# Row norms of an encoder layer gathered and spread by transposes instead of 32-bit matmuls, and two bank copies placed behind a third

## The chip, the cores and the metric

The kernel runs on one core of one Trainium2 chip. The metric is the device time of one launch in microseconds (us); for the kernel before there are three timed runs, with a median of 1317.9 us (1316.01 to 1318.08). One more execution was recorded by the hardware profiler. Engines in the profile: PE (the matrix engine, with its weight loads as PEld), DVE (vector), ACT (scalar), POOL (GpSimd) and SP (whose queue issues nearly all DMAs).

## The reference

One layer of an encoder, 1024 tokens of width 1024, in 32-bit floats. Cut to what matters here:

```
def rms_norm(x, g):
    y = x * rsqrt(mean(x * x, axis=-1) + 1e-6)
    return y * g

h = rms_norm(x, norm_mix)
q_a, k_a, v_a, q_b, k_b, v_b, g_a, g_b = split(h @ w_in)
o_a = neighbourhood_attention(...)      # 8 heads of 64
o_b = sliding_window_attention(...)     # 8 heads of 64, 2 key/value heads
y = sigmoid(g_a) * (o_a @ w_branch_a) + sigmoid(g_b) * (o_b @ w_branch_b)
x = x + y @ w_out
h = rms_norm(x, norm_ffn)
u = silu(h @ w_gate) * (h @ w_up)       # width 2816
x = x + u @ w_down
```

What the change touches are the two norms. Each needs one factor `rsqrt(mean + eps)` per token. The factor is not applied to `x` ahead of the matmul; it multiplies the product, whose tokens lie along the free axis of a tile, so that the factor must stand in all 128 partitions.

## The kernel before, in words

Activations are kept transposed: features in the 128 partitions, tokens along the free axis, in two halves of 512 tokens. A 32-bit product is made from three matmuls of a faster 32-bit type: each operand is split into a high and a low part (helper lines L50 and L51 for a plain split, L53 and L54 with a scale per partition; names end in h and l), and L824, L825 and L826 multiply high by high, high by low, low by high.

The stages follow one another on PE: projections, attention heads mixed with gate projections as filler, the other gates, the branch products, the output product (`out_pair`), the FFN's hidden blocks, the down product. From the gates on, a 2x2 block product is made of seven products instead of eight (class `Seven`, products named 1 to 7, taken in the order 1, 5, 6, 2, 7, 3, 4, and for the hidden blocks 0 and 1 in the order 1, 5, 6, 7, 3, 2, 4). The operand of a product p is a sum of weight blocks (s1 to s4, added by DVE at L806) that is then split; PSUM banks X, Y, Z and V (two sets, 0 and 1) accumulate it. When product 1 and then product 6 are done, ACT copies a bank into another (L828), from which later products go on.

**The norms.** `wide_rs` holds the factor for the 512 tokens of a half in all 128 partitions. For the first norm, the factors of all tokens come from ACT and POOL as columns `rows_rs` (128 tokens by 8). `wide_norm`, called twice within the filler, has DVE multiply the identity by each of four columns (`diag`), and PE multiply a tile of ones by the four diagonal matrices (L161); ACT copies the bank into `wide_rs`. For the second norm, `both_sums` (the same tile as `wide_rs`) holds squares summed over the 8 feature tiles; `ffn_norm` adds up its partitions with matmuls against one column of ones (L1227), DVE scales (L1229), POOL raises to the power -0.5 (L1230). `diagonal` and `spread_norm` (L1236, L1241) then do for it what `wide_norm` does for the first. On PE the gather stands behind product 6 of the hidden blocks 0 and 1, then come 24 matmuls of product 7 of both blocks into the banks Z, then the spread; bank V serves for the gathered sums and then for the spread factors.

**Hidden blocks.** `hidden(i)`, i from 0 to 21, makes 128 columns of the gate and of the up product for all tokens, two blocks at a time from i = 4. `p5` is a copy of bank V (after product 5), `c22` the sum of bank Z and `p5` (after product 7, L1364). DVE and ACT then apply the norm and the gating (`gated`, L1246 to L1248, and L1366 to L1370). From block 4 on, product 1 of a pair is itself made from seven products over quarters (`first_products`, L1318 to L1320; operands named sq, qa to qd, tokens q and qb), while product 5 of both blocks is woven in between, so that `hidden` is told that 5 is `given`. `first_products` ends with a copy of bank X of the second block into its bank Y (L1346), kept as `att["first"]`.

**What sets the order.** The order on PE is written out in the program. ACT, DVE, POOL and SP get theirs from the scheduler of the framework, which works with a simulated time line, except in an opening and in a stretch from the last output product to the spread of the second norm (`begin` to `change.close()`), where ACT and DVE also follow the program. `tc.issue_after(x)` makes the scheduler put what follows behind x. A small edit can therefore move rows on ACT, DVE and SP far from its own place.

Of the kernel before, what the change touches and what calls it, by code (L numbers as in the profile page):

```python
# [10 lines left out]
F32 = mybir.dt.float32  # L11
F32R = mybir.dt.float32r
AF = mybir.ActivationFunctionType
ALU = mybir.AluOpType
AX = mybir.AxisListType

T = 1024
D = 1024
# [3 lines left out]
EPS = 1e-6  # L22
# [3 lines left out]
def block_kernel(ctx, tc, x, xt, small, w_in, rpb, t5, w_ba, w_bb, w_out, w_gate, w_up, w_down,  # L26
                 onehot, swmask, namask, out):
    nc = tc.nc
    P = 128

    cst = ctx.enter_context(tc.tile_pool(name="cst", bufs=1))
    big = ctx.enter_context(tc.tile_pool(name="big", bufs=1))
    wp = ctx.enter_context(tc.tile_pool(name="wp", bufs=1))
# [23 lines left out]
    NWU = 8  # L57
# [29 lines left out]
    def half_cols(h):  # L87
        return slice(h * 512, h * 512 + 512)
# [3 lines left out]
    def halves(z):  # L92
        return z[:, LO], z[:, HI]
# [8 lines left out]
    def tok(t):  # L102
        return slice(t * P, (t + 1) * P)


    ident = cst.tile([P, P], F32, name="ident")
# [9 lines left out]

    ones = cst.tile([P, P], F32, name="ones")
    nc.gpsimd.memset(ones, 1.0)  # L120
    h = [[None, None] for k in range(8)]
    for e, c in ((0, 1), (0, 0), (1, 0), (1, 1)):
        for k in range(e, 8, 2):
# [3 lines left out]
    rows_rs = cst.tile([P, 8], F32, name="rows_rs")  # L127
# [18 lines left out]
    def row_norm(c):  # L146
# [5 lines left out]
        nc.gpsimd.tensor_scalar(rows_eps[:, d], rows_rs[:, d], HD * EPS, 1.0, op0=ALU.mult, op1=ALU.mult)  # L152
        nc.gpsimd.tensor_tensor(rows_rs[:, d], rows_rs[:, d], mhalf[:, 0:4], ALU.pow)

    def wide_norm(c, ps):

        dg = wp.tile([P, 512], F32, tag="whi", name=f"diag{c}", bufs=NWU)
        for j in range(4):
            nc.vector.tensor_scalar_mul(dg[:, tok(j)], ident, rows_rs[:, 4 * c + j:4 * c + j + 1])
        for j in range(4):  # L160
            nc.tensor.matmul(ps[:, tok(j)], ones, dg[:, tok(j)], start=True, stop=True)  # L161
        nc.scalar.copy(wide_rs[c], ps)

    def load_small():
# [61 lines left out]
    att = {}  # L226
# [230 lines left out]
    def filler(pending):  # L457
        for gi in range(1, len(order)):
            for i, cost in enumerate(projection(gi, weights[gi], pending, weights.get(gi + 1))):
                if gi == len(order) - 1 and i == 58:  # L460
                    wg = gate_weights(1, 0)
                yield cost
        todo = [(0, 1), (1, 1), (0, 0), (1, 0)]
        for i, (d, br) in enumerate(todo[:3]):
            def step(half, k):
                if i == 0 and not half and k in (1, 4):
                    wide_norm(k // 4, bank("pj", f"wide{k}"))
                if (i, half, k) == (1, 0, 0):
                    load_pair(0, slot_v, dma)
                at_step = 16 * i + 8 * half + k  # L470
                if at_step == 32:
                    load_pair(1, slot_v, dma)
                if at_step in range(26, 34) or at_step in range(40, 48):
                    if at_step in (26, 40):
                        j = at_step // 40
                        g22 = early.setdefault("g22", slot_u("g22h") if not j else None)
                        early[j] = row_sums(j, halves(g22)[j])
                    with tc.issue_after(att["bound"]):
                        next(early[at_step // 40])
                if (half, k) == (0, 7):  # L480
                    step.next = gate_weights(*todo[i + 1][::-1])
                if (half, k) in ((0, 6), (1, 3), (2, 1)):
                    pop(pending)
            yield from plain_gate(d, br, wg, step)
            wg = step.next
        last_gate.append(wg)
# [264 lines left out]
    def scratch(nm):  # L751
        return hp.tile([P, 512], F32, tag="S", name=nm, bufs=2)
# [4 lines left out]
    def scratch2(nm):  # L757
        return hp.tile([P, 1024], F32, tag="e4", name=nm, bufs=4)
# [14 lines left out]
    def bank_sets():  # L773

        return [{b: bank(t, f"bank{b}{i}") for b, t in zip("XYVZ", tags)}
                for i, tags in enumerate((("s", "pj", "s", "pj"), ("t", "pj", "t", "o")))]
# [130 lines left out]
    sets = bank_sets()  # L907
# [74 lines left out]
    sets = bank_sets()  # L982
# [13 lines left out]
    for n, (d, half) in enumerate(turns):  # L996
        j, c = d // 2, half_cols(half)
# [17 lines left out]
        if half == 0:  # L1015
            p = 2 if d % 2 else 1
# [37 lines left out]
    def prefetch_ffn(i):  # L1054

        if i >= NF:
            return prefetch_down(i - NF)
        st = [w_stage(f"wg{i}_"), w_stage2(f"wu{i}_")]
        for t, w in zip(st, (w_gate, w_up)):
            dma(t.rearrange("p (k c) -> p k c", c=P), w[0, :, tok(i)].rearrange("(k p) c -> p k c", p=P))  # L1060
        hid[i] = Seven(f"f{i}", [two(z) for z in st], 4, mx, sets)
# [28 lines left out]
    both_sums = wide_rs  # L1090
# [14 lines left out]
    def feed(*what):  # L1105

        for n, j in what:
            hi, lo = mx[BACK[n]][j]
            src, scale = raw_t[j][BACK[n]]
            split(hi, lo, src if kept(n, j) else f(lo), scale=scale)  # L1110
# [113 lines left out]
    def ffn_norm(half, ss):  # L1224

        for j in range(4):
            nc.tensor.matmul(ss[:, j:j + 1], both_sums[half][:, tok(j)], ones[:, 0:1], start=True, stop=True)  # L1227
        rs = hp.tile([P, 4], F32, tag="rs", name=f"rs{half}", bufs=2)
        nc.vector.tensor_scalar(rs, ss[:, 0:4], 1.0 / D, EPS, op0=ALU.mult, op1=ALU.add)  # L1229
        nc.gpsimd.tensor_tensor(rs, rs, mhalf[:, 0:4], ALU.pow)  # L1230
        return rs

    def diagonal(half, rs):
        dg = scratch(f"dg{half}")
        for j in range(4):
            nc.vector.tensor_scalar_mul(dg[:, tok(j)], ident, rs[:, j:j + 1])  # L1236
        return dg

    def spread_norm(half, dg, rb):
        for j in range(4):  # L1240
            nc.tensor.matmul(rb[:, tok(j)], ones, dg[:, tok(j)], start=True, stop=True)  # L1241
        nc.scalar.copy(rsb[half], rb)

    def gated(dst, src, half):

        nc.vector.tensor_mul(dst, src, rsb[half])  # L1246
        nc.scalar.activation(dst, dst, AF.Silu)  # L1247
        att["two"] = nc.vector.tensor_mul(dst, dst, rsb[half]).ins  # L1248
# [100 lines left out]
    def hidden(i, order=ORDER, given=()):  # L1349

        s = hid[i]
        us[i] = scratch2(f"u{i}")
        sg_lo, sg_hi = halves(us[i])
        p5, c22 = halves(scratch2(f"p5{i}"))
        y, z, v = (s.banks[b] for b in "YZV")
        for p in order:
            if p not in given:
                s.step(p)
            if p == 2:
                gated(sg_lo, s.banks["X"], 0)  # L1360
            elif p == 5:
                nc.scalar.copy(p5, v)
            elif p == 7:
                att["two"] = nc.vector.tensor_add(c22, z, p5).ins  # L1364
            elif p == 3:
                nc.vector.tensor_add(sg_hi, y, p5)  # L1366
                gated(sg_hi, sg_hi, 1)
            elif p == 4:
                nc.vector.tensor_mul(sg_lo, z, sg_lo)
                att["two"] = nc.vector.tensor_mul(sg_hi, c22, sg_hi).ins  # L1370
                if i % 2:
                    keep(i // 2, us[i - 1], us[i])
            if p == order[3]:
                prefetch_ffn(i + 2)
            yield p

    def keep(k, u0, u1):

        (b11, b12), (b21, b22) = halves(u0), halves(u1)
        t = TokenSums(f"u{k}", b11, b12, b22).rest(b21)  # L1380
        for n, p in enumerate(ORDER):
            row = (7 * k + n) * P
            nc.sync.dma_start(u_dram[row:row + P, :], t[p][0])

    ga, gb = (hidden(i, LAST2) for i in range(2))

    def both_blocks():
        next(ga)
        next(gb)
# [10 lines left out]
    for i, g in enumerate((ga, gb)):  # L1400
        prepare_ffn((i, 3))
        next(g)
    rs = [ffn_norm(half, sets[half]["V"]) for half in range(2)]
    feed(*((4, j) for j in range(4)))
    dg = [diagonal(half, rs[half]) for half in range(2)]
    both_blocks()
    prepare_ffn((0, 2), (1, 2))
    for half in range(2):
        spread_norm(half, dg[half], sets[half]["V"])
    feed(*((5, j) for j in range(4)))  # L1410
    change.close()
    in_turn(ga, gb)
# [1 line left out]
    for _ in hidden(2):  # L1414
        next(pieces)
    g = hidden(3)
    for p in g:
        next(pieces, None)
        if p == 3:
            break  # L1420
    for i in range(4, NF, 2):

        first = first_products(hid[i], hid[i + 1])
# [112 lines left out]
```

## Time and profile before

| | |
|---|---|
| timed runs | 1317.9, 1316.01, 1318.08 us |
| the profiled execution | 1317.18 us |
| its span, first to last instruction | 1315.2 us |
| mean granted clock of TensorE | 0.999 |
| PE busy | 1304.1 us, 99% of the span |
| DVE busy | 1018.6 us, 77% |
| ACT busy | 695.5 us, 53% |
| POOL busy | 182.8 us, 14% |

The span leaves out 2 us before the first and after the last instruction. Busy shares are averages: DVE is at nine tenths and more in some slices of the span and at half in others. Matmuls overlap in their pipeline, so a row of the time line gives the start of the first of a group, and the next row's start tells what the group cost.

### The profile page before, as it was taken

To read this page: it belongs to the slowest core of one execution; us is meant where nothing else is said; L and a number is where in the kernel's file an instruction comes from. 1 tells how busy PE (TensorE), PEld (TensorE's weight loads), DVE (VectorE), ACT (ScalarE), POOL (GpSimd) and SP (SyncE) were. 2 spreads that over 40 slices of the span, in tenths; PEclk is the share of its full clock that TensorE was granted. 3 is DMA by queue.
4 is the path that set the end of the run, shared out by engine and by line. 5 is a ranking of instruction groups with operands and counts; after the bars stand their busy time and mean duration, and the time that the engine had idled before them with its cause. 6 is when DMAs were issued, how large, how long until landed. Compare 5 with 4: busy or idle time off the path is not lost.

```text
span 1315.2 us, 19621 instructions
## 1 busy us (share of the span) xinstructions
PE 1304.1 (99%) x6618; PEld 1134.0 (86%) x6618; DVE 1018.6 (77%) x2039; ACT 695.5 (53%) x1459; POOL 182.8 (14%) x322
## 2 busy tenths in 40 slices
PE   9999999999999999999999999999999999999998
PEld 8999999999888888888888888888888888888887
DVE  5678867776687758879999878888777799697765
ACT  6677857776664225535556544443444455363532
POOL 1364645564310000000000000000000000000000
PEclk9999999999999999999999999999999999999999
DMA  9532424242535358657774533233233356672532
GB/s 311 147 89 61 110 62 109 61 135 64 143 118 184 122 158 275 216 188 220 253 235 120 168 105 106 87 104 117 80 109 121 120 171 221 240 248 65 184 121 88
DMA packets 180997, 191.92 MB, mean 146 GB/s; under 512 B 21104, under 2 KB 126576, under 8 KB 180896
## 3 DMA queue, kind: packets, MB, share of 16 engines
q1 hardware_dynamic: 180640, 190.57, 46.5%
q8 instruction: 52, 0.85, 0.3%
q14 instruction: 49, 0.40, 0.1%
q10 hardware_dynamic: 256, 0.10, 0.0%
HBM read 133.19 MB, written 52.37 MB: 141 GB/s over the span
## 4 chain that ended last, share of the span: by engine, by line
PE 84%; DMA 7%; DVE 5%; ACT 2%; issue 1%; SPq 1%; POOL 1%; POOLq 0%; ACTq 0%; DVEq 0%
PE bankZ L824 5%; PE bankZ L825 5%; PE bankZ L826 5%; PE bankY L824 5%; PE bankY L825 5%; PE bankY L826 5%; PE bankX L826 4%; PE bankX L824 4%; PE bankX L825 4%; PE pj L326 4%; PE pj L325 4%; PE pj L327 4%; PE o L649 3%; PE bankV L825 3%; PE bankV L824 3%; PE bankV L826 3%
## 5 line engine op out<-in xcount | busy, mean ns | idle before, releaser
L603 ACT ACTIVATE E<-E,nm 128x384 f32<-128x384 f32 (+3 forms) x128 | 75.7, 592 | 48.3 <-DVE nm L597 42.5
L605 POOL TENSOR_SCALAR E<-E,nm 128x384 f32<-128x384 f32 (+1 forms) x128 | 74.5, 583 | 95.0 <-DVE nm L604 71.0
L51 DVE TENSOR_TENSOR pl<-tp,ph 128x384 fp32r<-128x384 f32 (+1 forms) x128 | 66.4, 519 | 17.2 <-ACT ph L50 16.1
L50 ACT CAST ph<-tp 128x384 fp32r<-128x384 f32 (+1 forms) x128 | 57.4, 449 | 20.4 <-PE tp L615 19.9
L50 ACT CAST f<-f 128x512 fp32r<-128x512 f32 x87 | 50.9, 620 | 25.5 <-DMA f<-u_dram 24.9
L51 DVE TENSOR_TENSOR f<-f 128x512 fp32r<-128x512 f32 x87 | 56.4, 683 | 8.3 <-ACT f L50 8.1
L615 PE MATMUL tp<-ident,E 128*128 128x128 f32 x352 | 59.5, 272 | 0.9 <-POOL E L605 0.9
L615 PEld LDWEIGHTS tp<-ident,E 128*128 128x128 f32 x352 | 45.1, 140 | 5.9 <-POOL E L605 1.2
L345 POOL TENSOR_TENSOR ss<-ss,mhalf 128x4 f32<-128x4 f32 (+2 forms) x42 | 49.8, 1185 | 3.2
L649 PE MATMUL o<-pl,v 128*128 128x256 f32 (+2 forms) x160 | 48.7, 305 | 0.4 <-DVE pl L51 0.3
L604 DVE RECIPROCAL nm<-nm 128x1 f32<-128x1 f32 x128 | 20.4, 160 | 36.0 <-ACT E L603 34.6
L1230 POOL TENSOR_TENSOR rs<-rs,mhalf 128x4 f32<-128x4 f32 x2 | 2.8, 1419 | 319.1 <-DVE rs L1229 319.1
L649 PE MATMUL o<-ph,v 128*128 128x256 f32 (+2 forms) x160 | 45.9, 301 | 0.5 <-ACT ph L50 0.5
L591 PE MATMUL s<-k,q 128*128 128x384 f32 (+1 forms) x128 | 46.0, 359 | 0.0
L592 PE MATMUL s<-k,q 128*128 128x384 f32 (+1 forms) x128 | 41.4, 323 | 0.0
L597 DVE CUSTOM_DVE_ANT_0 E<-s,bsw,cols 128x384 f32<-128x384 f32 (+1 forms) x64 | 36.9, 577 | 4.6 <-PE s L592 3.9
L1247 ACT ACTIVATE u<-u 128x512 f32<-128x512 f32 x44 | 27.5, 629 | 19.7 <-DVE u L1246 19.6
L597 DVE CUSTOM_DVE_ANT_0 E<-s,bna 128x384 f32<-128x384 f32 (+1 forms) x64 | 32.9, 516 | 4.3 <-PE s L592 3.8
L824 PE MATMUL bankZ<-f,f_7h 128*128 128x512 f32 x88 | 35.0, 397 | 0.8 <-ACT bankZ L828 0.8
L1248 DVE TENSOR_TENSOR u<-u,wide_rs 128x512 f32<-128x512 f32 x44 | 30.0, 686 | 6.4 <-ACT u L1247 5.6
L826 PE MATMUL bankZ<-f,f_7l 128*128 128x512 f32 x88 | 34.7, 395 | 0.0
L825 PE MATMUL bankZ<-f,f_7h 128*128 128x512 f32 x88 | 34.7, 394 | 0.0
(1268 smaller groups left out, 4636.0 us busy)
## 6 DMA issues: line engine op xcount, KB each, us to landing
f<-u_dram SPq DMA_DIRECT2D x77, 256.0 KB
wg_s<-in_w_gate_dram SPq DMA_DIRECT2D x22, 512.0 KB
u_dram<-u SPq DMA_DIRECT2D x33, 256.0 KB
o_dram<-of SPq DMA_DIRECT2D x32, 256.0 KB
o<-o_dram SPq DMA_DIRECT2D x32, 256.0 KB
sg<-g_dram SPq DMA_DIRECT2D x32, 256.0 KB
g_dram<-go SPq DMA_DIRECT2D x24, 256.0 KB
u_dram<-tau SPq DMA_DIRECT2D x22, 256.0 KB
```

The costliest lines, as they stand in the source:

```text
L50: a = nc.scalar.copy(hi, src)
L51: b = (eng or nc.vector).tensor_tensor(lo, src, f(hi), ALU.subtract)
L325: nc.tensor.matmul(ps[:, :384], lh, his[k][:, :384], start=(k == 0), stop=False)
L326: nc.tensor.matmul(ps[:, :384], lh, los[k][:, :384], start=False, stop=False)
L597: att["bound"] = nc.vector.tensor_tensor_reduce(E[:, :n], s[:, :n], hd["bias"](qb), -1.0, sk if sw else 1e30, ALU.add, ALU.min, nm[:, 0:1] ...
L603: nc.scalar.activation(E[:, :m], E[:, :m], AF.Exp, bias=nm[:, 0:1], scale=-1.0, accum_out=nm[:, 1:2])
L605: nc.gpsimd.tensor_scalar(E[:, :n], E[:, :n], nm[:, 1:2], 1.0, op0=ALU.mult, op1=ALU.mult)
L615: nc.tensor.transpose(tp[:, tok(j)], hd["E"][qq][:, ko:ko + P], ident)
L649: nc.tensor.matmul(hd["O"][half][:, (a - half * 4) * P:(z + 1 - half * 4) * P], v[:, kb].rearrange("p a e -> p (a e)"), pp[:, (a - q0) * P ...
L824: nc.tensor.matmul(ps, hi[:, tok(j)], bh, start=first, stop=False, skip_group_check=True)
L825: nc.tensor.matmul(ps, hi[:, tok(j)], bl, start=False, stop=False, skip_group_check=True)
L826: nc.tensor.matmul(ps, lo[:, tok(j)], bh, start=False, stop=end, skip_group_check=True)
```

## The change

Three edits in the program.

1. The `ones` tile and its memset on POOL are gone. A new helper `spread` makes four 32-bit transposes: each takes one column of factors, read with stride 0 as a 128x128 matrix, so that the transpose puts the 128 factors of that column into every partition. `wide_norm` and `spread_norm` call it in place of diagonal matrices and matmuls. DVE's 8 `diag` and 8 `dg` multiplications are gone.
2. `ffn_norm` transposes the four 128x128 pieces of `both_sums` into the whole of bank V, and DVE adds up each 128 columns (`tensor_reduce`, 128x512 in, 128x4 out) ahead of the scaling. POOL's power stays.
3. In `hidden`, where product 5 is given (blocks 4 to 21), the copy of bank V into `p5` is issued after `att["first"]`.

```diff
-    ones = cst.tile([P, P], F32, name="ones")
-    nc.gpsimd.memset(ones, 1.0)
...
+    def spread(ps, rs):
+
+        for j in range(4):
+            nc.tensor.transpose(ps[:, tok(j)], rs[:, j:j + 1].to_broadcast([P, P]), ident)
+
     def wide_norm(c, ps):
 
-        dg = wp.tile([P, 512], F32, tag="whi", name=f"diag{c}", bufs=NWU)
-        for j in range(4):
-            nc.vector.tensor_scalar_mul(dg[:, tok(j)], ident, rows_rs[:, 4 * c + j:4 * c + j + 1])
-        for j in range(4):
-            nc.tensor.matmul(ps[:, tok(j)], ones, dg[:, tok(j)], start=True, stop=True)
+        spread(ps, rows_rs[:, 4 * c:4 * c + 4])
         nc.scalar.copy(wide_rs[c], ps)
...
     def ffn_norm(half, ss):
 
         for j in range(4):
-            nc.tensor.matmul(ss[:, j:j + 1], both_sums[half][:, tok(j)], ones[:, 0:1], start=True, stop=True)
+            nc.tensor.transpose(ss[:, tok(j)], both_sums[half][:, tok(j)], ident)
         rs = hp.tile([P, 4], F32, tag="rs", name=f"rs{half}", bufs=2)
-        nc.vector.tensor_scalar(rs, ss[:, 0:4], 1.0 / D, EPS, op0=ALU.mult, op1=ALU.add)
+        nc.vector.tensor_reduce(rs, ss.rearrange("p (j c) -> p j c", c=P), axis=AX.X, op=ALU.add)
+        nc.vector.tensor_scalar(rs, rs, 1.0 / D, EPS, op0=ALU.mult, op1=ALU.add)
         nc.gpsimd.tensor_tensor(rs, rs, mhalf[:, 0:4], ALU.pow)
         return rs
 
-    def diagonal(half, rs):
-        dg = scratch(f"dg{half}")
-        for j in range(4):
-            nc.vector.tensor_scalar_mul(dg[:, tok(j)], ident, rs[:, j:j + 1])
-        return dg
-
-    def spread_norm(half, dg, rb):
-        for j in range(4):
-            nc.tensor.matmul(rb[:, tok(j)], ones, dg[:, tok(j)], start=True, stop=True)
+    def spread_norm(half, rs, rb):
+        spread(rb, rs)
         nc.scalar.copy(rsb[half], rb)
...
             elif p == 5:
-                nc.scalar.copy(p5, v)
+                with ExitStack() as line:
+                    if given:
+                        line.enter_context(tc.issue_after(att["first"]))
+                    nc.scalar.copy(p5, v)
```

On PE every row keeps its place; only the four groups of matmuls above become transposes. The other engines' rows move. Numbers behind names are the program's; line numbers of the changed kernel are some 7 lower from the FFN on.

ACT in a pair of hidden blocks (8 and 9), before: the two copies of bank V (L1362) stand ahead of the split of the second block's weights for product 7 and of the copy into bank Y1 (L1346).

```order
L50 CAST f8_7h_9663<-s3f8_9357 128x512
L1341 COPY bankY0_6640<-bankX0_6639 128x512
L1362 COPY p58_9584<-bankV0_6641 128x512
L1362 COPY p59_9587<-bankV1_6645 128x512
L50 CAST f9_7h_9689<-s3f9_9383 128x512
L1346 COPY bankY1_6644<-bankX1_6643 128x512
```

The same place of the changed kernel:

```order
L50 CAST f8_7h_9643<-s3f8_9337 128x512
L1334 COPY bankY0_6628<-bankX0_6627 128x512
L50 CAST f9_7h_9669<-s3f9_9363 128x512
L1339 COPY bankY1_6632<-bankX1_6631 128x512
L1358 COPY p58_9564<-bankV0_6629 128x512
L1358 COPY p59_9567<-bankV1_6633 128x512
```

The two copies of bank V moved behind the split and the copy into Y1; the same happens in the other eight pairs.

DVE ahead of `c22` of hidden block 3 (named p53 here, the sum of bank Z1 and p53), while the operands of the first quarter products (block 4) are made, before:

```order
L1307 TENSOR_TENSOR sq1f4_8786<-wg5_s_8734,wg4_s_8577 128x256
L1308 TENSOR_TENSOR sq1f4_8786<-wg4_s_8577,sq0f4_8785 128x256
L1246 TENSOR_TENSOR u3_8656<-bankX1_6643,wide_rs0_110 128x512
L51 TENSOR_TENSOR qcf4l_8865<-sq1f4_8786,qcf4h_8864 128x512
L51 TENSOR_TENSOR qdf4l_8896<-wg5_s_8734,qdf4h_8895 128x256
L806 TENSOR_TENSOR s1f4_8581<-wu4__8578 128x512
L1248 TENSOR_TENSOR u3_8656<-u3_8656,wide_rs0_110 128x512
L1269 TENSOR_TENSOR qb_8517<-qb_8517,qt2_8590 128x2x256
L1364 TENSOR_TENSOR p53_8657<-bankZ1_6646,p53_8657 128x512
```

and now:

```order
L1239 TENSOR_TENSOR u3_8636<-bankX1_6631,wide_rs0_108 128x512
L1297 TENSOR_TENSOR sq0f4_8765<-wg4_s_8557,sq0f4_8765 128x256
L1241 TENSOR_TENSOR u3_8636<-u3_8636,wide_rs0_108 128x512
L1262 TENSOR_TENSOR qb_8497<-qb_8497,qt2_8570 128x2x256
L51 TENSOR_TENSOR qbf4l_8821<-sq0f4_8765,qbf4h_8820 128x512
L1300 TENSOR_TENSOR sq1f4_8766<-wg5_s_8714,wg4_s_8557 128x256
L1301 TENSOR_TENSOR sq1f4_8766<-wg4_s_8557,sq0f4_8765 128x256
L1360 TENSOR_TENSOR p53_8637<-bankZ1_6634,p53_8637 128x512
```

The three rows of the gating of block 3 and of qb moved up, and the low parts qcf4l and qdf4l and the sum s1f4 moved behind the sum with bank Z1.

DVE in the first blocks of the down product, where the split of the weights for product 6 (d0_6l, d1_6l) stands among the gating of blocks 20 and 21 and the splits of the activations (f4_0 to f4_3), before:

```order
L51 TENSOR_TENSOR f4_2_8163<-f4_2_8163 128x512
L51 TENSOR_TENSOR f4_3_8165<-f4_3_8165 128x512
L1370 TENSOR_TENSOR u20_11563<-p520_11564,u20_11563 128x512
L51 TENSOR_TENSOR d0_6l_11959<-s2d0_11666,d0_6h_11958 128x512
L806 TENSOR_TENSOR s2d1_11692<-wda1s_11687,s1d1_11691 128x512
L1370 TENSOR_TENSOR u21_11566<-p521_11567,u21_11566 128x512
L838 TENSOR_TENSOR tau10_11773<-u20_11563 128x512
L842 TENSOR_TENSOR tbu10_11774<-u20_11563,u21_11566 128x512
L51 TENSOR_TENSOR d1_6l_11977<-s2d1_11692,d1_6h_11976 128x512
```

and now:

```order
L51 TENSOR_TENSOR f4_2_8151<-f4_2_8151 128x512
L1366 TENSOR_TENSOR u20_11543<-p520_11544,u20_11543 128x512
L51 TENSOR_TENSOR f4_3_8153<-f4_3_8153 128x512
L1366 TENSOR_TENSOR u21_11546<-p521_11547,u21_11546 128x512
L51 TENSOR_TENSOR d0_6l_11939<-s2d0_11646,d0_6h_11938 128x512
L805 TENSOR_TENSOR s2d1_11672<-wda1s_11667,s1d1_11671 128x512
L837 TENSOR_TENSOR tau10_11753<-u20_11543 128x512
L841 TENSOR_TENSOR tbu10_11754<-u20_11543,u21_11546 128x512
L840 TENSOR_TENSOR tau10_11753<-tau10_11753,u21_11546 128x512
L51 TENSOR_TENSOR d1_6l_11957<-s2d1_11672,d1_6h_11956 128x512
```

One more row of the gating stands ahead of d0_6l, and one row of the token sums (tau10) ahead of d1_6l.

More of the change, by code (lines that the diff above doesn't have):

```diff
@@ L1404, in block_kernel @@
     feed(*((4, j) for j in range(4)))
-    dg = [diagonal(half, rs[half]) for half in range(2)]
     both_blocks()
@@ L1408, in block_kernel @@
     for half in range(2):
-        spread_norm(half, dg[half], sets[half]["V"])
+        spread_norm(half, rs[half], sets[half]["V"])
     feed(*((5, j) for j in range(4)))
```

## The prediction

> **What bounds the kernel.** I read the page first, then the list of waits on PE, then stretches and the time line at each place that the change touches.
>
> ```profile
> span 1315.2 us, 19621 instructions
> PE 1304.1 (99%) x6618; PEld 1134.0 (86%) x6618; DVE 1018.6 (77%) x2039; ACT 695.5 (53%) x1459; POOL 182.8 (14%) x322
> PE 84%; DMA 7%; DVE 5%; ACT 2%; issue 1%; SPq 1%; POOL 1%; POOLq 0%; ACTq 0%; DVEq 0%
> ```
>
> PE is busy for all but 11 us, and 84% of the chain that ended last is PE. So what PE no longer executes is gained, unless PE then waits. From the list of waits on PE (total us, times, longest) and a stretch of the hidden blocks (PE, PEld, DVE, ACT, POOL busy, clock, DMA share, GB/s):
>
> ```profile
> PE tp L615 <- POOL E L605: 0.9, 1, 0.9
> PE bankZ L824 <- ACT bankZ L828: 0.8, 1, 0.8
> ...
> 830.00:1080.00 250.00, 250.00 (x1241) 212.59 (x1240) 199.21 (x337) 111.06 (x207) 0.00 (x0) 1.00 0.36 113
> ```
>
> The first wait is in the attention, the second lies between the gather and the spread of the FFN's norm. Over 250 us of hidden blocks PE never waits. The sum goes against the profiled execution: 1317.18 us, 2 us above its span. The median of three is 1317.9, the mean of all four executions 1317.3; I take 1317.3. About 0.2%, 2.6 us, is what a measurement of this kernel can tell from no change.
>
> **The first norm.** PE's time line, and two stretches of the 26 transposes at the start of the kernel:
>
> ```profile
> 330.15 1.05 PE L161 MATMUL wide<-diag,ones 128*128 128x128 f32 x8
> 330.96 0.42 PE L649 MATMUL o<-ph,v 128*128 128x384 f32 x1
> ...
> 334.07 1.05 PE L161 MATMUL wide<-diag,ones 128*128 128x128 f32 x8
> 334.88 0.47 PE L427 MATMUL pg<-h,wg_1h 128*128 128x512 f32 x1
> ...
> 1.50:3.60 2.10, 2.10 (x10) 2.10 (x11) 1.00 0.82 235
> 4.84:5.93 1.09, 1.09 (x12) 1.09 (x10) 1.00 0.71 158
> ```
>
> Four 32-bit matmuls are eight records; the next instruction starts 0.81 us after the first of them, so each call costs PE 0.81. A transpose of the same size is one record. The start shows 10 in 2.10 us, then 12 that touch 1.09 us; taking off the two that overlap its ends, 0.109 each once warm. Four cost 0.44. Two calls save 2 x (0.81 - 0.44) = 0.75 us. The transpose reads its column with stride 0, which no row shows; between 0.44 and the matmuls' 0.81 I take 0.44, the row of the same operation. DVE loses the eight `diag` rows; none of them ended a wait of PE, so I cost that at nothing.
>
> Can the 0.75 be eaten? DVE is dense some 30 us later (columns as above):
>
> ```profile
> 370.00:380.00 10.00, 9.08 (x50) 7.50 (x49) 7.98 (x23) 5.68 (x16) 2.35 (x5) 1.00 0.70 237
> ```
>
> There PE has its 0.9 us wait, behind DVE and POOL. If DVE's backlog does not move with PE, the wait grows by 0.75 and the gain is zero. But the work in it is fed by attention scores from PE and by loads that the program ties to PE's steps, so it moves along. I take the full 0.75 and keep 0 as the end.
>
> **The gather and the spread of the FFN's norm.** PE, the clock's stretch, DVE, and groups of POOL and DVE:
>
> ```profile
> 695.60 1.84 PE L1227 MATMUL bankV<-ones,wide_rs 128*128 128x1 f32 x16
> 698.26 0.80 PE L824 MATMUL bankZ<-f,f_7h 128*128 128x512 f32 x1 [0.82 <-ACT bankZ L828]
> ...
> 705.19 1.95 PE L1241 MATMUL bankV<-dg,ones 128*128 128x128 f32 x16
> 706.89 0.47 PE L824 MATMUL bankY<-f,f_3h 128*128 128x512 f32 x1
> ...
> 697.75:701.16 3.41, 2.90 (x7) 2.31 (x8) 3.41 (x6) 3.41 (x7) 0.00 (x0) 0.50 0.03 11
> ...
> 701.21 0.22 DVE L1229 TENSOR_SCALAR rs<-bankV 128x4 f32<-128x4 f32 x2
> ...
> 704.00 1.65 DVE L1236 TENSOR_SCALAR dg<-ident,rs 128x128 f32<-128x128 f32 x8
> 705.57 1.27 DVE L1364 TENSOR_TENSOR p<-bankZ,p 128x512 f32<-128x512 f32 x2
> ...
> L1230 POOL TENSOR_TENSOR rs<-rs,mhalf 128x4 f32<-128x4 f32 x2 | 2.8, 1419 | 319.1 <-DVE rs L1229 319.1
> L337 DVE TENSOR_REDUCE ss<-qn x48: 400/415/490, 29.4 to 330.0; 128x4 f32<-128x256 f32 x32, 128x5 f32<-128x320 f32 x16
> ```
>
> The gather's eight transposes cost 0.87 instead of 1.84, but PE then waits for ACT's copy of bank Z until 698.26 whatever the gather took: the 0.97 turns into wait, gain 0. The spread takes 706.89 - 705.19 = 1.70 and will take 8 x 0.109 = 0.87: gain 0.83, if the factors are there.
>
> They come like this. DVE reaches the norm at 701.21. A reduction of 128x512 has no row; from 0.40 for 256 columns and 0.49 for 320 I estimate 0.70. With 0.15 for the scaling: rs0 at 702.06, rs1 at 702.91; POOL, 1.42 each, finishes rs0 at 703.48 and rs1 at 704.90. PE arrives at 705.19 as before: no wait. DVE has 1.40 us more (two reductions) and 1.65 less (`dg`): L1364 comes 0.25 earlier.
>
> Between 698.26 and 705.19 the 24 matmuls take 6.93 us, for the clock is at 0.50 from 697.75 to 701.16; at the 0.227 us of a warm matmul (the busy stretch above holds 250.00 / 1241 = 0.20 for its mixed shapes) they would take 5.4. If the dip vanished, PE would be at the spread at 703.7, wait for rs1 until 704.90, and f_3 would start at 705.35: a gain of 1.5, not of 2.3.
>
> The row says what counts as work for the clock: transposes alone, from 1.50 on, brought the pitch from 0.21 to 0.11. The Trainium skill, "TensorE: Matmul & The Clock Gate", Part 4, states the opposite, that transposes do not count as busy for the gate; this trace disagrees, with the 0.21 and the 0.11. By that rule PE would look idle from 695.60 to 698.26 and the dip would stay or grow (a rival below); by the row it stays or goes, and the sum below is the same for both, since something else binds next: 1315.6 either way, and by the rule with a grown dip 1317.3.
>
> **What binds next.** At the first quarter products PE already waits for `c22` of block 3; rows of PE, DVE and, from the chain, of loads of up-weights (us from issue to landing):
>
> ```profile
> 759.28 0.28 PE L1320 MATMUL bankV<-f,qaf4l 128*128 128x256 f32 x1
> 759.70 0.50 PE L824 MATMUL bankZ<-f,f_4h 128*128 128x512 f32 x1
> ...
> 740.53 0.69 DVE L51 TENSOR_TENSOR f_7l<-s3f,f_7h 128x512 fp32r<-128x512 f32 x1 [0.96 <-ACT f_7h L50]
> ...
> 745.35 0.68 DVE L51 TENSOR_TENSOR f_4l<-wu__8352,f_4h 128x512 fp32r<-128x512 f32 x1
> ...
> 758.96 0.68 DVE L1364 TENSOR_TENSOR p<-bankZ,p 128x512 f32<-128x512 f32 x1
> ...
> 746.06 3.97 DMA wu__8735<-in_w_up_dram
> 708.67 5.46 DMA wu__8331<-in_w_up_dram
> 669.75 8.38 DMA wu__7961<-in_w_up_dram
> ```
>
> L1320's pitch is 0.12, so PE could have gone on at 759.40 and lost 0.30. In the new order five rows that stood ahead of `c22` (q-operands, s1f4) stand behind it or elsewhere, but four rows of gating and qt/qa move ahead of f3_4l. That is 4 x 0.60 = 2.4 us, less some 0.9 of DVE's idle at 740.53 that they fill: f3_4l ends at 747.5. It frees the buffer for the load of block 5's up-weights, whose landing is 751.5 instead of 750.03. From s1f5 on, ten rows lead to the end of `c22`: seven of 0.60 and four of 0.34 make 5.6, a wait for ACT's cast of f5_5h (0.6 to 1.0, since nothing stands between s1f5 and f5_5l now) makes 6.3 to 6.9: 757.8 to 758.4, against 759.64. I take 758.4. So the gains of this stretch end at 759.70 - 758.45 = 1.25 at most, and PE needs 0.83 + 0.30 = 1.13 of it. I take 1.15 for the FFN's norm; with no dip it would be 1.25.
>
> **The copies of bank V.** ACT, PE and the reader of `p5`, in the pair of blocks 8 and 9:
>
> ```profile
> 847.62 1.07 ACT L1362 COPY p<-bankV 128x512 f32<-128x512 f32 x2 [0.98 <-PE bankV L826]
> 848.58 0.63 ACT L50 CAST f_7h<-s3f 128x512 fp32r<-128x512 f32 x1
> 849.10 0.60 ACT L1346 COPY bankY<-bankX 128x512 f32<-128x512 f32 x1
> ...
> 850.88 0.39 PE L824 MATMUL bankY<-f,f_6h 128*128 128x512 f32 x1
> ...
> 862.84 0.68 DVE L1364 TENSOR_TENSOR p<-bankZ,p 128x512 f32<-128x512 f32 x1
> ```
>
> The copy into Y1 ends at 849.70, 1.2 us before PE needs it at 850.88; it may come 1.0 earlier. The V copies come 1.1 later, with 13 us until L1364. Nine pairs x 0 = 0.
>
> **The down product.** Each operand of product 6 stands one DVE row (0.60) later:
>
> ```profile
> 1111.21 0.68 DVE L51 TENSOR_TENSOR d_6l<-s2d,d_6h 128x512 fp32r<-128x512 f32 x1
> 1112.72 0.39 PE L824 MATMUL bankY<-f,d_6h 128*128 128x512 f32 x1
> ...
> 1114.22 0.68 DVE L51 TENSOR_TENSOR d_6l<-s2d,d_6h 128x512 fp32r<-128x512 f32 x1
> 1115.44 0.39 PE L824 MATMUL bankY<-f,d_6h 128*128 128x512 f32 x1
> ```
>
> Ready 0.8 and 0.5 us ahead now; PE, some 1.9 us earlier, pulls its own token sums along, but not all of DVE. 0.6 later leaves 0.2 and -0.1, so between 0 and 0.7 is lost; I take 0.2. The memset of `ones` on POOL falls away at no price: PE's start waits for the identity.
>
> **The sum.** 0.75 + 1.15 - 0.2 = 1.7 us. 1317.3 - 1.7 = 1315.6 us, 0.13% less.
>
> **Rivals.**
> *Everything sticks, and nothing binds.* The dip goes, POOL's factors are just in time, `c22` too: 0.75 + 1.5 + 0.3 = 2.55, and 0.75 + 2.3 + 0.3 = 3.35 if POOL's factors come 0.8 earlier than its rows say: 1314.75 to 1313.95. For it: five rows fewer ahead of `c22`. Against it: rs1 at 704.90.
> *The gain is eaten.* DVE's backlog at 376 takes the 0.75, and `c22` or an operand in the down product the rest: 1316.7 to 1317.9. For it: DVE is 7.98 of 10 us busy there, and a load that lands in 5.2 instead of 3.97 us already puts `c22` back to 759.64.
> *The dip grows.* By the page's rule, a second stretch of 3.41 us at half clock costs half of its work, 1.7 us; 1.15 becomes -0.55 and the time 1317.3. Against it: the pitch at the start.
> *Slower.* The up-weights of block 5 land like those of block 1, in 8.4 us: 755.9, `c22` at 762.8, PE waits till then, 3.1 us later than before. The sum is 1317.3 + 3.1 + 0.2 = 1320.6. It decides from 5.2 us on for no gain, from 7.8 for 2.6 us lost. Against it: the 8.38 was measured where DMA was busiest.
>
> **How the numbers follow.** Forecast 0.45, everything sticks 0.22, eaten 0.19 and the grown dip 0.05, slower 0.09. Executions of one kernel differ by 2 us here, medians by about 1. Under 1314.7 lies most of the second case (0.18) and the tail of the first (0.17): faster 0.35. Slower is the last case and a rest of the eaten one: 0.10. Same 0.55. The range reaches from 1313.2 (the second case, less its spread) to 1318.2 (the eaten gain and its spread) and leaves out the slower case and the tails; the forecast's own is 1314.4 to 1316.8.
>
> **What would show it.** Right: L161's successor with 4 records and 0.44; the wait for bank Z near 1.7 instead of 0.82; 8 records of the spread within 0.9 and no wait for POOL ahead of it; no wait at the first quarter products; the hidden blocks still at 250.00. Wrong: a stretch at 0.50 longer than 3.41 us, the wait at L615 above 1.5, a wait behind DVE at 759 or 1112, or a PE gap in a place that I did not look at.

## The result and the profile after

The changed kernel took 1313.78 us in the median of 16 runs (1312.43 to 1315.32), the kernel before 1315.62 (1313.91 to 1318.08, also 16). The ratio is 0.9985, with a 95% interval of 0.9978 to 0.9992: 1.84 us less, where 1.7 had been forecast. The four executions that the forecast started from were on the slow side; the kernel before is some 1.7 us faster than their mean of 1317.3, and that, not the change, is why the absolute time lies near the lower end of the range, 1.8 us under the forecast of 1315.6 and outside the forecast's own 1314.4 to 1316.8.

The page of the changed kernel, its list of waits on PE, and the hidden blocks as a stretch:

```profile
span 1312.4 us, 19559 instructions
PE 1301.0 (99%) x6594; PEld 1130.9 (86%) x6594; DVE 1014.9 (77%) x2025; ACT 695.0 (53%) x1459; POOL 180.4 (14%) x321
PE 88%; DMA 5%; DVE 3%; ACT 2%; SPq 1%; issue 1%; POOL 1%; ACTq 0%; DVEq 0%; POOLq 0%
...
PE bankY L823 <- ACT bankY L1334: 0.9, 1, 0.9
PE tp L614 <- POOL E L604: 0.9, 1, 0.9
PE bankZ L823 <- ACT bankZ L827: 0.6, 1, 0.6
...
830.00:1080.00 250.00, 250.00 (x1241) 212.61 (x1240) 198.38 (x337) 113.04 (x210) 0.00 (x0) 1.00 0.36 117
```

PE is busy for 3.1 us less and the span is 2.8 us shorter. One wait is new in the list: 0.9 us for a copy into bank Y. Lines of the changed kernel are a few lower: L156 is `spread`, L1226 the gather, L823 to L825 the product, L1334 the copy into Y0, L1360 `c22`.

The first norm, on PE's time line:

```profile
330.85 0.60 PE L156 MATMUL wide<-ident,rows_rs 128*128 128x128 f32 x4
331.21 0.42 PE L648 MATMUL o<-ph,v 128*128 128x384 f32 x1
...
334.30 0.60 PE L156 MATMUL wide<-ident,rows_rs 128*128 128x128 f32 x4
334.66 0.48 PE L426 MATMUL pg<-h,wg_1h 128*128 128x512 f32 x1
```

Four transposes with a stride of 0 cost 0.36 instead of 0.81: 0.9 us for both calls, 0.15 more than forecast.

The norm of the FFN: PE, the reduction on DVE, POOL's power, and the stretch of time that was at half clock in the profile before (in the order PE, PEld, DVE, ACT, POOL, clock, DMA share, GB/s).

```profile
695.37 1.04 PE L1226 MATMUL bankV<-ident,wide_rs 128*128 128x128 f32 x8
697.00 0.50 PE L823 MATMUL bankZ<-f,f_7h 128*128 128x512 f32 x1 [0.59 <-ACT bankZ L827]
702.59 1.26 PE L156 MATMUL bankV<-ident,rs 128*128 128x128 f32 x8
703.61 0.47 PE L823 MATMUL bankY<-f,f_3h 128*128 128x512 f32 x1
...
L1228 DVE TENSOR_REDUCE rs<-bankV x2: 683/688/693, 699.9 to 700.7; 128x4 f32<-128x512 f32 x2
...
L1230 POOL TENSOR_TENSOR rs<-rs,mhalf x2: 1017/1105/1193, 701.0 to 702.0; 128x4 f32<-128x4 f32 x2
...
697.75:701.16 3.41, 3.41 (x16) 2.79 (x16) 3.38 (x7) 3.41 (x7) 0.19 (x1) 1.00 0.00 0
```

The spread takes 1.02 instead of 1.70 (0.2 of it between the fourth and the fifth transpose, which starts at 703.21, just after POOL's second power ends), the reduction 0.69 as estimated, POOL 1.1 instead of 1.4. The clock is 1.00 throughout here, and the 24 matmuls between take 5.6 us instead of 6.93.

I followed the same instructions of PE through all profiles, from mark to mark (us; a mark is the time in the profile of the kernel before). The second column of the kernel before is the experiment below that has its exact order of instructions on all engines and no stretch at half clock:

| from mark to mark | before | before's order, full clock | after |
|---|---|---|---|
| first product to 312.2 | 305.51 | 306.30 | 306.28 |
| 329.9 to 335.2, first norm | 5.26 | 5.26 | 4.35 |
| 358.0 to 380.1, attention | 22.10 | 21.97 | 22.60 |
| 380.1 to 657.7, gates to output product | 277.64 | 277.25 | 277.14 |
| 695.4 to 698.26, gather and wait | 2.89 | 3.07 | 1.86 |
| to 705.0, product 7 | 6.69 | 5.34 | 5.36 |
| to 706.89, spread | 1.94 | 2.53 | 1.25 |
| to 759.7, the first quarter products | 52.81 | 52.49 | 52.52 |
| to 810.6, pair of blocks 6 and 7 | 50.91 | 50.79 | 51.71 |
| to 1101.9, the other blocks | 291.22 | 291.26 | 291.22 |
| to 1129.9, start of the down product | 28.11 | 28.11 | 28.11 |

The stretches between these rows agree within 0.04. Up to 312.2, in the attention and from 380.1 to 657.7 the same row differs from one profile to another by up to 1.2, 0.9 and 1.8 us, whatever the kernel: the changed kernel has 277.14, 276.74 and 278.24 in the last of them. The other rows repeat within some hundredths where no wait differs.

### The profile page after: what moved, and what is told of

Its sections match the earlier page's. It is cut to its first block, busy times and chain, and to the rows that moved or that the text cites. A ratio compares the mean times of both kernels' runs of the same rounds, so it can differ in the third digit from the quotient of the medians.

```text
span 1312.4 us, 19559 instructions
## 1 busy us (share of the span) xinstructions
PE 1301.0 (99%) x6594; PEld 1130.9 (86%) x6594; DVE 1014.9 (77%) x2025; ACT 695.0 (53%) x1459; POOL 180.4 (14%) x321
## 4 chain that ended last, share of the span: by engine, by line
PE 88%; DMA 5%; DVE 3%; ACT 2%; SPq 1%; issue 1%; POOL 1%; ACTq 0%; DVEq 0%; POOLq 0%
PE bankZ L823 6%; PE bankZ L824 6%; PE bankZ L825 6%; PE bankY L823 6%; PE bankY L824 6%; PE bankY L825 6%; PE bankX L823 4%; PE bankX L825 4%; PE bankX L824 4%; PE pj L324 4%; PE pj L325 4%; PE pj L326 4%; PE o L648 3%; PE bankV L824 3%; PE bankV L823 3%; PE bankV L825 3%
## 5 line engine op out<-in xcount | busy, mean ns | idle before, releaser
L50 ACT CAST f_5h<-s1f 128x512 fp32r<-128x512 f32 x22 | 13.7, 622 | 41.7 <-DVE s1f L805 36.4
L823 PE MATMUL bankY<-f,f_6h 128*128 128x512 f32 x88 | 34.5, 392 | 0.9 <-ACT bankY L1334 0.9
L823 PE MATMUL bankZ<-f,f_7h 128*128 128x512 f32 x88 | 34.4, 390 | 0.6 <-ACT bankZ L827 0.6
L824 PE MATMUL bankV<-f,f_5h 128*128 128x512 f32 x88 | 34.4, 391 | 0.0
```

Source lines behind the costliest of these rows:

```text
L50: a = nc.scalar.copy(hi, src)
L823: nc.tensor.matmul(ps, hi[:, tok(j)], bh, start=first, stop=False, skip_group_check=True)
L824: nc.tensor.matmul(ps, hi[:, tok(j)], bl, start=False, stop=False, skip_group_check=True)
```

## The experiments

"Theory A" is the prediction's: what PE no longer executes counts, until a wait takes it back. "Theory B" came from the second look at the pair of blocks 6 and 7. The ratios are to the kernel before on the same chip, with 95% intervals.

**The first norm alone.**

```diff
-        dg = wp.tile([P, 512], F32, tag="whi", name=f"diag{c}", bufs=NWU)
...
-            nc.tensor.matmul(ps[:, tok(j)], ones, dg[:, tok(j)], start=True, stop=True)
+        spread(ps, rows_rs[:, 4 * c:4 * c + 4])
```

> The kernel before with only the first norm's spread as transposes (its 8 diag rows on DVE gone); the norm of the FFN and the copies as before. Theory A (PE's own work counts): the two calls cost 0.35 each instead of 0.81, so PE is 0.9 us earlier at 335 us; about 0.5 is lost again in a wait behind DVE at 360 us, and some 0.4 to 0.9 is left from 500 us on: ratio to the kernel before 0.9993 to 0.9997. Rival (DVE and POOL bind the attention's end): all of it is lost by 380 us and the ratio is 1.0000. At 698 us the half-clock stretch is as before.

Measured 0.9990 (0.9982 to 0.9999), 1314.26 against 1315.78, a little more than expected. The 0.91 of PE are there and are not eaten: the wait behind `pl` near 360 us, which I had taken for the price, is 0.3 in all here, but 0.8 in the next experiment, which leaves this norm as it was; it varies by itself. And this kernel, with the old gather of 128x1 matmuls, has no dip of the clock and no wait behind the gather:

```profile
695.88 1.84 PE L1228 MATMUL bankV<-ones,wide_rs 128*128 128x1 f32 x16
697.58 0.48 PE L825 MATMUL bankZ<-f,f_7h 128*128 128x512 f32 x1
...
703.51 2.05 PE L1242 MATMUL bankV<-dg,ones 128*128 128x128 f32 x16 [0.20 <-DVE dg L1237]
```

**The spread of the FFN's norm alone** (gather by matmuls, `spread_norm` by `spread`, no `diagonal`).

> The kernel before with only the spread of the FFN's norm as transposes (8 dg rows on DVE gone); gather and first norm as before, copies as before. Theory A: the spread costs 0.87 instead of 1.70, PE is 0.8 us earlier at 706 us, and the wait at the first quarter products shrinks or stays, so that 0.8 to 1.1 is left: ratio 0.9992 to 0.9994. If the half-clock stretch is not the gather's doing but a matter of phase, it may be there or not in the profile; if the gather of 128x1 matmuls and the wait behind it cause it, it stands at 698 us as in the kernel before.

Measured 0.9996 (0.9988 to 1.0005): less than expected, and not told from no change by time. In its profile the spread is short and waits for nothing, as forecast:

```profile
703.05 1.03 PE L158 MATMUL bankV<-ident,rs 128*128 128x128 f32 x8
703.84 0.47 PE L829 MATMUL bankY<-f,f_3h 128*128 128x512 f32 x1
```

0.79 for eight transposes. Five of its 12 executions had a granted clock under 1.000, and they hold the slow end of its range (up to 1318.2): the median of the other seven is 1314.33. The executions of the kernel before at 1.000 on that chip have 1315.62, so that like against like 1.3 us are gained, more than theory A's 0.8 to 1.1. This comparison was made afterwards.

**The gather with full columns**, to see what the clock's gate takes for work.

```diff
-            nc.tensor.matmul(ss[:, j:j + 1], both_sums[half][:, tok(j)], ones[:, 0:1], start=True, stop=True)
+            nc.tensor.matmul(ss[:, tok(j)], both_sums[half][:, tok(j)], ones, start=True, stop=True)
```

> The kernel before with one thing changed: the gather multiplies by all 128 columns of ones instead of one column, so that the same 16 matmul records stream 128 columns each (128x128 instead of 128x1); the order of all engines is the same. Theory A (the clock counts columns that stream through PE): the half-clock stretch at 698 us goes, PE reaches the spread some 1.4 us earlier and then waits for dg behind POOL and DVE until about 705.5, so the time stays within 0.3 us: ratio 0.9997 to 1.0002, and the mean granted clock of the runs is 1.000 where the kernel before has 0.999. Rival (the clock counts idle time, or the phase of its window decides): the stretch at half clock is still there in most runs.

Measured 1.0003 (0.9994 to 1.0011). PE in its profile:

```profile
695.93 1.95 PE L1227 MATMUL bankV<-ones,wide_rs 128*128 128x128 f32 x16
698.76 0.50 PE L824 MATMUL bankZ<-f,f_7h 128*128 128x512 f32 x1 [0.89 <-ACT bankZ L828]
...
704.83 2.05 PE L1241 MATMUL bankV<-dg,ones 128*128 128x128 f32 x16 [0.33 <-DVE dg L1236]
```

No dip, and then the wait for `dg` that the expectation had put in its place. But one profile is no proof that streamed columns keep the clock up. Of the thirteen profiles only that of the kernel before has the dip; five others have the 128x1 gather too and are without it. The mean granted clock of the other executions does not count the dips either. One stretch of 3.41 us at half clock takes 3.41 x 0.5 / 1315 = 0.0013 off the mean, which prints as 0.999, but so prints half a clock in the last 1.4 us of the span, when PE has finished. That is all that the three other profiles at 0.999 have, here one of the changed kernel:

```profile
1309.70:1311.10 1.40, 0.00 (x0) 0.00 (x0) 0.00 (x0) 0.00 (x0) 0.00 (x0) 0.50 0.00 0
```

At 0.998 and below more than 3.9 us were at half clock, longer than the 3.7 us from PE's last matmul to the end of the span, so these executions had a dip while PE worked. Of the kernel before they are 8 of 82 (10 more are at 0.999 and can be either), and their median is 1.2 to 2.8 us above that of the executions at 1.000 on the same chip. Over all kernels with the 128x1 gather they are 13 of 129 (leaving out one at 0.949 that took no longer than its neighbours), and none of 79 with the gather by transposes (68) or by full columns (11). So the dip is an event of single executions, and its odds seem to hang on the form of the gather, as theory A has it; no run was made to separate this from the rest, and the mechanism stays open.

**The changed kernel without the copies' edit.**

```diff
-                with ExitStack() as line:
-                    if given:
-                        line.enter_context(tc.issue_after(att["first"]))
-                    nc.scalar.copy(p5, v)
+                nc.scalar.copy(p5, v)
```

> The changed kernel without its third edit (the copies of bank V stand where the scheduler puts them), both norms by transposes. By the prediction the copies are worth nothing: the same as the changed kernel, ratio 0.9985 to the kernel before. Rival: without the edit the scheduler now puts both V copies of blocks 6 and 7 ahead of the copy into bank Y0, which PE already awaits at 807 us in the changed kernel for 0.94 us; two copies of 0.52 make that wait 1.5 to 2.0 us and the ratio 0.9990 to 0.9993. If the 0.94 us came from the copies' edit itself, the wait would be gone here and the ratio 0.9978.

Measured 0.9987 (0.9978 to 0.9996), 1314.09, 0.3 above the changed kernel and within both intervals. ACT and PE, pair of blocks 6 and 7:

```profile
805.72 1.07 ACT L1355 COPY p<-bankV 128x512 f32<-128x512 f32 x2
806.68 0.60 ACT L1334 COPY bankY<-bankX 128x512 f32<-128x512 f32 x1
...
807.33 0.50 PE L823 MATMUL bankY<-f,f_6h 128*128 128x512 f32 x1 [1.71 <-ACT bankY L1334]
```

The V copies stand ahead of the copy that PE waits for, and the wait is 1.71 instead of 0.94. Two more profiles of the changed kernel, below, have 0.7, so the edit saves 0.8 to 1.0 of waiting at this one pair; in the time 0.3 is seen, which the noise covers.

**Both spreads, old gather, no copies' edit.** (`ffn_norm` and `p5` as in the kernel before, with `ones`.)

> Both spreads as transposes (wide_norm and the FFN's), the gather still by 128x1 matmuls with ones, no edit of the copies; DVE, ACT and SP then keep the order of the kernel before from block 5 on. Theory B: of the change's gain, 1.2 us are given back at 807 us, because the scheduler's new order lets block 5's f5_4l and so the load of block 7's up-weights come later; where the old order stands, PE does not wait there. PE saves 0.91 at the first norm, 0.8 and the wait for dg at the spread, nothing is given back: ratio 0.9978 to 0.9984, 0.2 to 0.9 us under the changed kernel. Rival: the gather by transposes brings the 1.0 us that the traces show between 695 and 698 us; then this kernel is 0.3 to 1.0 us above the changed one, ratio 0.9987 to 0.9992.

Measured 0.9978 (0.9969 to 0.9987), 1312.19. PE passes from the quarter products to product 6 of block 6 without the wait: 50.51 from 759.7 to 810.6, where the changed kernel has 51.46 to 51.71. Beside it on the same chip:

> The changed kernel once more, beside the others on one chip: ratio 0.9985 within 0.0005; a wait of 0.8 to 1.3 us at bank Y near 807 us if it belongs to the order of the instructions, none if it was one slow load of that execution.

Measured 0.9988 (0.9979 to 0.9997), 1313.16. The wait belongs to the order of the instructions: it is there again, with 0.7 instead of the expected 0.8 to 1.3. The two spreads alone are 1.0 us under the changed kernel, though the intervals overlap. The repeat also shows the other wait that was forecast, in the down product:

```profile
PE bankY L823 <- ACT bankY L1334: 0.7, 1, 0.7
PE bankY L825 <- DVE d_6l L51: 0.5, 1, 0.5
```

The start of the down product takes 29.18 there instead of 28.11. In the two other profiles of the changed kernel that operand was ready in time.

**The gather alone** (transposes and reductions; spreads by diagonal matrices).

> The kernel before with only the gather as transposes and reductions on DVE; spreads by diagonal matrices as before. Theory A: the 0.97 us that PE saves turn into a longer wait for ACT's copy of bank Z, and dg comes 1.3 us later (two reductions ahead), so PE waits for it at the spread for up to 1.5: ratio 1.0000 to 1.0006. Rival (the copy is there earlier, since the whole of ACT and DVE moves with PE): 0.9993.

Measured 1.0024 (1.0015 to 1.0033): 3.4 us slower in the median, more than either theory had. Theory A's direction holds. PE, and one row of its list of waits:

```profile
705.22 2.05 PE L1247 MATMUL bankV<-dg,ones 128*128 128x128 f32 x16 [1.79 <-DVE dg L1242]
...
PE bankZ L829 <- DVE p L1370: 0.8, 1, 0.8
```

With two reductions of 0.69 ahead of POOL and the eight `dg` rows behind it, PE waits 1.79 at the spread and 0.8 for a later `c22`. From mark to mark these two stretches take 2.4 to 2.9 us more than with the old gather, and the gather itself 0.3 less; what is left of the 3.4 was not traced.

**The copies alone.**

> The kernel before with only the third edit: copies of bank V behind the copy into Y1 in the nine pairs, norms as before. Theory A: 0, ratio 0.9998 to 1.0002, PE without waits from 830 to 1080 us. Rival: the new order of DVE and SP from block 6 to the down product makes new waits (d0_6l, d1_6l, up-weights): up to 1 us slower, ratio 1.0004 to 1.0008.

Measured 1.0035 (1.0023 to 1.0046): 4.3 us slower, four times what the rival had allowed. From its list of waits, and the worst place:

```profile
PE bankV L826 <- DVE d_5l L51: 1.2, 1, 1.2
PE bankX L1318 <- ACT bankX L1329: 0.8, 2, 0.6
...
1111.49 0.50 PE L826 MATMUL bankV<-f,d_5l 128*128 128x512 f32 x1 [1.23 <-DVE d_5l L51]
```

Against the kernel before, PE takes 1.0 more in the pair of blocks 6 and 7 (counted against the 50.51 of the experiments with the spreads alone), 0.9 more over the next blocks and 1.9 more at the start of the down product. An edit of nine pairs of copies re-ordered DVE from 788 to 1215 us.

**The changed kernel with one cast forced ahead.** Where does the 0.94 us wait come from? Read back in the changed kernel's profile: PE, ACT and DVE at the copy, then the load, then ACT two pairs earlier.

```profile
807.51 0.50 PE L823 MATMUL bankY<-f,f_6h 128*128 128x512 f32 x1 [0.94 <-ACT bankY L1334]
806.87 0.58 ACT L1334 COPY bankY<-bankX 128x512 f32<-128x512 f32 x1
...
786.69 0.69 DVE L805 TENSOR_TENSOR s1f<-wu__9028 128x512 f32<-128x512 f32 x1 [3.52 <-DMA wu__9028<-in_w_up_dram]
780.30 0.69 SPq L97 DMA_DIRECT2D wu__9028<-in_w_up_dram  x1
779.59 0.69 DVE L51 TENSOR_TENSOR f_4l<-wu__8715,f_4h 128x512 fp32r<-128x512 f32 x1
...
768.86 0.57 ACT L1339 COPY bankY<-bankX 128x512 f32<-128x512 f32 x1 [1.67 <-PE bankX L1313]
769.34 1.08 ACT L1358 COPY p<-bankV 128x512 f32<-128x512 f32 x2
770.29 0.64 ACT L50 CAST f_7h<-s3f 128x512 fp32r<-128x512 f32 x1
```

DVE waits 3.52 us for the up-weights of block 7, whose load could start only when f5_4l was through with the buffer; f5_4l stands in DVE's queue behind f4_7l, which needs the cast f4_7h, which ACT makes behind three copies, the first of which waits 1.67 us for PE. In the kernel before that cast stands ahead of them, and of the copy into Y0:

```profile
770.41 0.62 ACT L50 CAST f_7h<-s3f 128x512 fp32r<-128x512 f32 x1 [2.21 <-DVE s3f L806]
770.93 0.58 ACT L1341 COPY bankY<-bankX 128x512 f32<-128x512 f32 x1
771.84 1.07 ACT L1362 COPY p<-bankV 128x512 f32<-128x512 f32 x2 [0.33 <-PE bankV L826]
```

The edit:

```diff
+            if a.nm == "f4":
+                for p in (6, 2):
+                    a.prepare(p), b.prepare(p)
+                a.prepare(7)
+                line.enter_context(tc.issue_after(chain[0]))
             att["first"] = nc.scalar.copy(b.banks["Y"], xb).ins
```

> The changed kernel with one thing forced: in the pair of blocks 4 and 5, ACT makes the split f4_7h ahead of the copies into Y1 and of bank V, as in the kernel before (in the changed kernel it stands behind them). Theory B: that cast holds up DVE's f4_7l and all behind it to f5_4l, whose end lets the load of block 7's up-weights start; with the cast some 1.5 us earlier the load starts 1.5 us earlier and PE's wait at bank Y at 807 us falls from 0.7 to 1.1 us to 0.2 or less: 0.6 to 1.0 us under the changed kernel, ratio 0.9978 to 0.9983. Rival (the load is slow by itself, or DVE's rows between the load and the copy set the time): the wait stays within 0.3 us of the changed kernel's, ratio 0.9985 to 0.9988.

Measured 0.9970 (0.9959 to 0.9982), 1313.08 us, beside the changed kernel:

> The changed kernel beside the two others, for their comparison on one chip: ratio 0.9983 to 0.9990, a wait of 0.7 to 1.1 us at bank Y near 805 us.

which measured 0.9980 (0.9972 to 0.9989), 1314.36. The chain in the kernel with the early cast:

```profile
767.08 0.62 ACT L50 CAST f_7h<-s3f 128x512 fp32r<-128x512 f32 x1 [1.28 <-DVE s3f L805]
767.61 0.58 ACT L1345 COPY bankY<-bankX 128x512 f32<-128x512 f32 x1
777.58 0.37 SPq L97 DMA_DIRECT2D wu__9028<-in_w_up_dram  x1
782.84 0.69 DVE L805 TENSOR_TENSOR s1f<-wu__9028 128x512 f32<-128x512 f32 x1 [1.05 <-DMA wu__9028<-in_w_up_dram]
...
804.89 0.28 PE L1313 MATMUL bankX<-q,qdf6l 128*128 128x256 f32 x1
805.01 0.40 PE L823 MATMUL bankY<-f,f_6h 128*128 128x512 f32 x1
```

Counted from the mark at 759.7, so that the earlier arrival of PE in this execution drops out (us; the last column is the stretch from 759.7 to 810.6):

| | cast f4_7h | load issued | the sum s1 of block 7 starts | wait of PE | stretch |
|---|---|---|---|---|---|
| before | 10.7 | 22.36 | 28.78 | none listed | 50.91 |
| changed, three profiles | 14.2 | 24.04 to 24.17 | 30.30 to 30.56 | 0.7 to 0.9 | 51.46 to 51.71 |
| early cast | 12.3 | 22.84 | 28.10 | none | 50.51 |
| both spreads, two profiles | 10.4 | 22.23 | 27.27 and 27.50 | none | 50.51 |

The load follows the cast: the cast comes 1.8 us earlier, the load 1.2 to 1.3, and PE no longer waits. That far theory B's chain is shown. But s1 comes 2.2 to 2.5 earlier, for in this execution the load was used 5.3 us after its issue, in the changed kernel after 6.3 to 6.4, and the edit does not set that; with 6.3 a small wait might have been left. The edit also let some other rows of ACT and DVE change places up to 800 us. The medians differ by 1.3 us, PE's stretch by 1.0; the two intervals overlap, so the gain in time is less sure than its mechanism. (The kernel before had a median of 1316.64 on this chip, so all three ratios here came out under the expected ones; what counts is the comparison among the three.)

**Both spreads once more.**

> Both spreads as transposes, gather and copies as in the kernel before, once more: ratio 0.9975 to 0.9983, under the changed kernel by 0.5 to 1.2 us, no wait at bank Y near 806 us. If it is no better than the changed kernel here, its lead was that of one chip.

Measured 0.9969 (0.9956 to 0.9981), 1312.79: 1.6 us under the changed kernel on this chip, 1.0 on the other. PE at the place of the wait:

```profile
804.46 0.28 PE L1314 MATMUL bankX<-q,qdf6l 128*128 128x256 f32 x1
804.58 0.40 PE L825 MATMUL bankY<-f,f_6h 128*128 128x512 f32 x1
```

PE goes from the quarter products to product 6 at the pitch of the rows before. The two spreads without the rest of the change have a lower median than the changed kernel on both chips, but the intervals of the two overlap on each, and the early cast (1313.08) is not told from them.

## Why the prediction was right, point by point

- **The first norm, 0.75.** Right; 0.91, and kept. The case in which DVE's backlog eats it did not come: the waits in the attention vary without the edit too.
- **The gather, 0.** Right in kind. The traces of before and after seem to say 1.0 (2.89 against 1.86), but with the old gather 1.94 was measured in five profiles of kernels that did not wait behind it; against those the transposes save 0.1 to 0.6, and a wait of 0.1 to 0.6 follows them, not the 1.7 that had been named as a sign of being right. ACT's copy of bank Z was held in place in the prediction; in the changed kernel it came earlier.
- **The spread, 0.83.** 0.7 in the changed kernel. The signs asked for 0.9 at most and no wait for POOL; it was 1.02 with 0.2 of waiting. What I had not counted: with no dip the old spread waits for `dg` (its stretch takes 2.14 to 2.53 in three profiles, 1.94 with the dip), and that goes with `dg`.
- **The dip of the clock.** Right that it would hardly change the sum: it costs 1.35 in product 7 (6.69 against 5.34), and without it 0.6 comes back at the spread (2.53 against 1.94). Wrong in treating it as a property of every execution; it is in 8 to 18 of 82 of the kernel before. The Trainium skill, "TensorE: Matmul & The Clock Gate", Part 4, states that transposes do not count as busy for the clock gate, and here the traces disagree. In twelve of the thirteen profiles the clock rises, 2.9 to 5.4 us after the first transpose, before PE has executed anything but transposes. The rival of a grown dip, which followed from that statement, did not come: the clock is 1.00 through the transposes of the changed kernel.
- **What binds next, `c22` of block 3.** Wrong. `c22` was forecast to end at 758.4, at the earliest at 757.8; it starts at 754.80 and ends at 755.49, and PE goes on at the pitch:

```profile
754.80 0.69 DVE L1360 TENSOR_TENSOR p<-bankZ,p 128x512 f32<-128x512 f32 x1
...
756.01 0.28 PE L1313 MATMUL bankV<-f,qaf4l 128*128 128x256 f32 x1
756.13 0.40 PE L823 MATMUL bankZ<-f,f_4h 128*128 128x512 f32 x1
```

  The failed step is the rows that I moved by hand at 0.60 each while holding the rest of DVE in place. DVE's queue had moved with PE: the stretch from 706.89 to 759.7 takes 52.49 to 52.64 in eleven profiles, though PE enters it up to 5 us earlier in one than in another. (The rows do not add up either: ten are priced as seven and four, and 5.6 with 0.6 to 1.0 is 6.2 to 6.6, not 6.3 to 6.9. That moves the end by 0.1 to 0.3 us and not the outcome.) And the 0.30 us lost there was of that execution: the experiment with the same order of instructions does not have it. The limit of 1.25 on the FFN's norm, and with it the 1.15 of the sum, therefore rested on a bound that was not there; that the 1.15 is near what was gained is luck.
- **The copies, 0.** Wrong for the edit by itself (4.3 us lost), nearly right within the change (0.3 us, not resolved). The term was worked out on ACT alone, from the copies' own slack. What the scheduler does to the other queues because of such an edit had no term.
- **The down product, 0.2.** 0 in two profiles of the changed kernel, 1.07 in one, 0.5 of it the wait that was named.
- **The slower rival** named the mechanism that did take something back, an up-weights load that DVE waits for ahead of what PE needs, but at block 5. It came at block 7, for 0.7 to 0.9 us. The sign "a PE gap in a place that I did not look at" stood for exactly this.

So the sum came out for reasons that partly cancel, and its closeness is in part luck: 0.9 from the first norm and about 1.3 from the FFN's (695.4 to 706.89 takes 9.4 and 9.7 in the two profiles with the old norm there and no wait behind the gather, 8.0 to 8.5 in the three of the changed kernel), less 0.7 to 0.9 at 807 us and now and then 1.1 in the down product. That is 0.2 to 1.5; 1.84 was measured, with an interval of 1.1 to 2.9, so 0.3 us or more of the 1.84 has no term. Fewer dips may be part of it; no run shows that.

## What to carry to other kernels

Where a scheduler orders the queues, an edit is its instructions plus the new order of every other queue; take the part that pays and leave out the part that only moves rows: here two spreads by transposes had a lower median than the whole change on both chips. A wait on the bound engine is explained only when it is followed back to the queue where something was late, here over a copy, a DVE row, a load, a buffer and a cast 40 us earlier. And before a feature of a profile is given a price, see in other profiles whether it is there; a mean over the whole execution may have another cause.

## What the hardware showed that I had not expected

The clock fell to half for one stretch of 3.41 us with PE at work on both sides: PE was 99% busy over the span, and its longest wait at that place was 0.82 us. The experiment with full columns waited 0.89 at the same place and had no dip. The clock also falls to half at the very end, when PE has finished (the last 1.4 us of the profile shown above). Eight 32-bit matmuls of 128x1 cost PE nearly as much as eight of 128x128 (1.84 and 1.95 us for 16 records); eight transposes of 128x128 whose source is one column read with stride 0 took 0.79 where matmuls took 1.70.
